# Batched matmul, 32 x (512x1024)·(1024x768): the few-row transfers moved from the first store to the last row tile of the first x, which is transposed late

## The chip, the cores and the metric

One core of a Trainium2 chip. The metric is the device time of one execution in microseconds (us); most executions of a kernel agree within some 0.3%.

## The reference

```python
def setup_inputs():
    batch, m, k, n = 32, 512, 1024, 768
    return {"x": np.random.randn(batch, m, k).astype(np.float32),
            "weight": np.random.randn(batch, k, n).astype(np.float32)}

def reference(x, weight):
    return np.matmul(x, weight).astype(np.float32)
```

The kernel casts to bf16 on the way in. It has to read 168 MB and write 50 MB.

## The kernel before

PE is the matrix engine, DVE and ACT are the vector and scalar engines, POOL and SP issue transfers; sixteen DMA engines share the bytes of a transfer, and it has landed when the last share has. Each batch has four row tiles of 128 rows (MT = 4). A row tile is transposed on the PE, copied out by DVE, and multiplied. The first x is loaded in f32 from the SP queue; the other x in pairs, and all weights, are loaded with a cast from the POOL queue. "x of batches 5 and 6" below is one such pair. The parts that matter (cuts marked with `...`):

```python
w_pool = ctx.enter_context(tc.tile_pool(name="w", bufs=4))
x_pool = ctx.enter_context(tc.tile_pool(name="x", bufs=3))
xT_pool = ctx.enter_context(tc.tile_pool(name="xT", bufs=6))
out_pool = ctx.enter_context(tc.tile_pool(name="out", bufs=7))
...
def transpose_first(mt):
    xT = xT_pool.tile([P, JT, P, 2], BF16, name="xT")
    for h in range(2):
        pt = tpsum.tile([P, JT, P], F32, name="pt")
        for i in range(JT):
            nc.tensor.transpose(pt[:, i, :], x_first[:, mt, JT * h + i::KT], ident)
        nc.vector.tensor_copy(...)
    return xT
...
def store(b):
    cols = MT * N
    if b == SKEWED:                       # SKEWED = 0: the first store
        cols -= 512
        for first in range(0, 120, 20):
            for at in range(first, first + 4):
                rows = slice(at, first + 20, 4)
                nc.sync.dma_start(out_view[b, rows, cols:], outs[b][rows, cols:])
        nc.sync.dma_start(out_view[b, 120:, cols:], outs[b][120:, cols:])
    nc.gpsimd.dma_start(out=out_view[b, :, :cols], in_=outs[b][:, :cols])
...
x_first = x_pool.tile([P, MT, K], F32, name="x_sb")
nc.sync.dma_start(x_first, x_view[0])
load_w(0)
...                                       # ident
load_pair(1); load_w(1); load_w(2); load_pair(3)
for b in range(B):
    if b % 2 and b + AHEAD + 1 < B:       # AHEAD = 3
        ...
            load_pair(b + AHEAD + 1)
    if b + AHEAD < B:
        load_w(b + AHEAD)
    ...                                   # stores; transposes
    for pair in range(2):
        pm = banks()
        for half in range(2):
            matmuls(pm, half, xT[2 * pair + half], b, range(KT), False)
        evacuate(b, pair, pm)
```

POOL issues its transfers in this order, one after the other, each when its buffer is free. The third x pair needs the buffer of the first x; the weights of batch 4 need the buffer of the weights of batch 0.

Of the kernel before, what the change touches and what calls it, by code (L numbers as in the profile page):

```python
# [13 lines left out]
def kernel(  # L14
# [6 lines left out]
    nc = tc.nc  # L21
    B, M, K = x.shape
    _, _, N = weight.shape
    P = 128
    MT = M // P
    KT = K // P
# [3 lines left out]
    AHEAD = 3  # L30
    LATE = 4
    HELD = 3
    SKEWED = 0

    const = ctx.enter_context(tc.tile_pool(name="const", bufs=1))
    w_pool = ctx.enter_context(tc.tile_pool(name="w", bufs=4))
# [10 lines left out]
    x_view = x.rearrange("b (mi mo) k -> b mi mo k", mi=P)  # L47
    pair_view = x[1:B - 1].rearrange("(p r) (mi mo) k -> p (r mi) mo k", r=2, mo=2 * MT)
    out_view = out.rearrange("b (mi mo) n -> b mi (mo n)", mi=P)

    xs, ws, outs = {}, {}, {}

    def banks():
        return [mpsum.tile([P, 512], F32, name=f"pm{i}") for i in range(3)]

    def load_pair(b):

        xs[b] = x_pool.tile([P, 2 * MT, K], BF16, name="x_sb")
        nc.gpsimd.dma_start(out=xs[b], in_=pair_view[b // 2])  # L59

    def load_last():
        xs[B - 1] = x_pool.tile([P, MT, K], BF16, name="x_sb")
        nc.gpsimd.dma_start(out=xs[B - 1], in_=x_view[B - 1])  # L63

    def load_w(b):
        ws[b] = w_pool.tile([P, KT, N], BF16, name="w_sb")
        at = 0
        for n in CHUNKED.get(b, (KT,)):
            nc.gpsimd.dma_start(out=ws[b][:, at:at + n, :], in_=w_view[b, :, at:at + n, :])  # L69
            at += n  # L70
# [9 lines left out]
    def transpose_pair(b, mt):  # L80

        both = xT_pool.tile([P, 2, JT, P // 2, 2, 2], BF16, name="xT")
        for half in range(2):
            nc.vector.tensor_copy(  # L84
                both[:, :, :, :, half, :].rearrange("p b j i r -> p j b i r"),
                words(b, mt + MT * half).rearrange("p j (b i r) -> p j b i r", b=2, r=2),
            )
        return [both[:, r].rearrange("p j i h r -> p j (i h) r") for r in range(2)]

    def transpose_last(mt):  # L90
        xT = xT_pool.tile([P, JT, P, 2], BF16, name="xT")
        nc.vector.tensor_copy(  # L92
            xT.rearrange("p j m r -> p (j m r)"), words(B - 1, mt).rearrange("p j m -> p (j m)")
# [10 lines that stand above are left out]
            nc.vector.tensor_copy(  # L104
                xT[:, 2 * h:2 * h + 2].rearrange("p j m r -> p j r m"),
                pt.rearrange("p (j r) m -> p j r m", r=2),
            )
        return xT
# [8 lines left out]
    def matmuls(pm, half, xT, b, kos, together):  # L117
        for ko in kos:
            for i, (bank, at, off, size) in enumerate(SPLITS[half]):
                shares = half == 1 and i == 0  # L120
                nc.tensor.matmul(  # L121
                    pm[bank][:, at:at + size],
                    xT[:, ko // 2, :, ko % 2],
                    ws[b][:, ko, off:off + size],
                    start=(ko == 0 and not (together and shares)),
                    stop=(ko == KT - 1),
                    skip_group_check=together,
                )

    def evacuate(b, pair, pm):  # L130
        o = outs[b][:, pair * N2:(pair + 1) * N2]
        nc.scalar.copy(o[:, 0:512], pm[0])  # L132
        nc.vector.tensor_copy(o[:, 512:1024], pm[1])  # L133
        nc.scalar.copy(o[:, 1024:N2], pm[2])  # L134

    def store(b):
        cols = MT * N
        if b == SKEWED:

            cols -= 512  # L140
            for first in range(0, 120, 20):
                for at in range(first, first + 4):
                    rows = slice(at, first + 20, 4)
                    nc.sync.dma_start(out_view[b, rows, cols:], outs[b][rows, cols:])
            nc.sync.dma_start(out_view[b, 120:, cols:], outs[b][120:, cols:])
        nc.gpsimd.dma_start(out=out_view[b, :, :cols], in_=outs[b][:, :cols])  # L146

    with tc.manual_schedule():
        x_first = x_pool.tile([P, MT, K], F32, name="x_sb")
        nc.sync.dma_start(x_first, x_view[0])  # L150
        load_w(0)
        ident = const.tile([P, P], F32)
        make_identity(nc, ident)
        load_pair(1)
        load_w(1)
        load_w(2)
        load_pair(3)

        ready = {}
        pending = []  # L160
        for b in range(B):
            if b % 2 and b + AHEAD + 1 < B:
                if b + AHEAD + 1 == B - 1:
                    load_last()
                else:
# [3 lines that stand above are left out]
            if b <= B - LATE:  # L169
                if b > 0:  # L170
                    pending.append(b - 1)
                if b + AHEAD < B - HELD or b == B - LATE:
                    for at in pending:
                        store(at)
                    pending = []
            if b == B - 1:
                halves = [slice(pair * N2, (pair + 1) * N2) for pair in range(2)]
                nc.sync.dma_start(out_view[b - 1, :, halves[0]], outs[b - 1][:, halves[0]])
                for late in range(B - LATE, B - 2):
                    nc.sync.dma_start(out_view[late], outs[late])  # L180
                nc.sync.dma_start(out_view[b - 1, :, halves[1]], outs[b - 1][:, halves[1]])
            outs[b] = out_pool.tile([P, MT * N], F32, name="out_sb")
            if b == 0:
                xT = {mt: transpose_first(mt) for mt in range(MT)}
            elif b == B - 1:
                xT = {mt: transpose_last(mt) for mt in range(MT)}
            else:
                if b % 2:
                    for mt in range(MT):
                        ready[b, mt], ready[b + 1, mt] = transpose_pair(b, mt)  # L190
                xT = {mt: ready.pop((b, mt)) for mt in range(MT)}
            if b not in CHUNKED:
                for pair in range(2):
                    pm = banks()
                    for half in range(2):
                        matmuls(pm, half, xT[2 * pair + half], b, range(KT), False)
                    evacuate(b, pair, pm)
                continue
            pms = [banks() for _ in range(2)]
            at = 0  # L200
            for n in CHUNKED[b]:
                last = at + n == KT
                for mt in range(MT):
                    matmuls(pms[mt // 2], mt % 2, xT[mt], b, range(at, at + n), True)
                    if last and mt % 2 == 1:
                        pair = mt // 2
                        evacuate(b, pair, pms[pair])
                        if b == B - 1:
                            nc.sync.dma_start(out_view[b, :, halves[pair]], outs[b][:, halves[pair]])
                at += n  # L210
# [30 lines left out]
```

## Time and profile before

| | before |
|---|---|
| time, first three runs | 517.0 us (515.5 to 518.96) |
| span of the profiled execution, granted clock | 515.9 us, 0.942 |
| PE busy | 440.0 us, 85% |
| HBM traffic over the span | 423 GB/s |

The views that carry the argument stand in the prediction below. One more is needed: the timeline of the first 36 us of the kernel before, cut to three lines (start and length in us, engine, line, what, count, and in brackets the idle time of the engine before it and what ended it).

```profile
12.27 6.95 PE L103 MATMUL pt<-ident,x_sb 128*128 128x128 f32 x32 [12.27 <-DMA x_sb<-in_x_dram]
...
19.52 0.53 POOL L59 DMA_DIRECT2D x_sb<-in_x_dram  x1 [14.38 <-PE pt L103]
...
29.92 0.53 POOL L69 DMA_DIRECT2D w_sb<-in_weight_dram  x1 [9.87 <-PE pm L121]
```

The first x has landed at 12.3 us. When its last transpose is through, at 19.5 us, POOL issues the next x pair, and when batch 0 is multiplied, at 29.9 us, the weights of batch 4. At those two moments the loads issued by 5.1 us still have work for the DMA engines: the last of them lands at 56.4 to 58.1 us.

### The profile page before, as it was taken

Reading aid. Unit: us, or ns where it says so; the run is one execution under the profiler, and the core shown is the slowest. Engines: PE = TensorE matmul, PEld = TensorE weight load, DVE = VectorE, ACT = ScalarE, POOL = GpSimd, SP = SyncE. Lnnn points to the kernel's source line nnn. Section 1 sums busy time; section 2 is a strip of 40 time slices with the busy share of each in tenths; the row PEclk is TensorE's granted clock in tenths of the full one; section 3 lists DMA queues with packets and bytes.
Section 4 is the critical chain, followed back from the end, with each engine's and each line's share of the span. In section 5 each row is a group of like instructions: output and inputs, shape, how many; then the busy total and the mean of one; then the engine's idle time right before and its main releaser. Section 6 shows DMA issues by size and latency. Waiting matters only on the chain.

```text
span 515.9 us, 5853 instructions
## 1 busy us (share of the span) xinstructions
PE 440.0 (85%) x2576; PEld 279.6 (54%) x2576; DVE 129.9 (25%) x196; ACT 76.2 (15%) x129; POOL 43.8 (8%) x87
## 2 busy tenths in 40 slices
PE   0999969979799697996979979898797988999992
PEld 0665635646366364663646636464464644656661
DVE  0541412314132041320413204141041410404131
ACT  0012111111111111111111111111111111111211
POOL 3001000010000100001000010000001100011000
PEclk9999998989899798997999979999798997999998
DMA  8999999999999999999999999999999999999996
GB/s 255 217 219 215 221 255 293 211 279 274 272 283 211 283 268 275 279 213 293 260 273 273 224 295 246 280 278 235 299 233 275 279 250 300 214 277 215 289 426 276
DMA packets 12952, 135.63 MB, mean 263 GB/s; under 512 B 1536, under 2 KB 1536, under 8 KB 3328
## 3 DMA queue, kind: packets, MB, share of 16 engines
q0 software_dynamic: 11664, 126.62, 96.2%
q1 hardware_dynamic: 1264, 8.65, 4.2%
q8 instruction: 20, 0.33, 0.2%
q14 instruction: 4, 0.03, 0.0%
HBM read 167.77 MB, written 50.33 MB: 423 GB/s over the span
## 4 chain that ended last, share of the span: by engine, by line
PE 64%; DMA 21%; DVE 7%; another core or an unknown queue 6%; issue 1%; ACT 0%
PE pm L121 56%; DMA w_sb<-in_weight_dram 19%; PE pt L77 6%; DVE xT L84 4%; DMA x_sb<-in_x_dram 2%; DVE out_sb L133 2%; PE pt L103 1%; DVE xT L104 0%; DVE xT L92 0%; ACT out_sb L134 0%
## 5 line engine op out<-in xcount | busy, mean ns | idle before, releaser
L121 PE MATMUL pm<-w_sb,xT 128*128 128x256 bf16 (+1 forms) x2048 | 358.9, 339 | 43.3 <-DMA w_sb<-in_weight_dram 43.3
L121 PEld LDWEIGHTS <-xT 128*128 128x128 bf16 x2048 | 206.8, 101 | 190.8 <-DMA w_sb<-in_weight_dram 47.9
L133 DVE COPY out_sb<-pm 128x512 f32<-128x512 f32 x64 | 44.3, 691 | 351.4 <-PE pm L121 338.4
L77 PE MATMUL pt<-ident,x_sb 128*128 128x128 f32 x496 | 79.8, 302 | 10.5 <-DVE xT L84 10.2
L132 ACT COPY out_sb<-pm 128x512 f32<-128x512 f32 x64 | 37.5, 585 | 305.9 <-PE pm L121 290.7
L77 PEld LDWEIGHTS pt<-ident,x_sb 128*128 128x128 f32 x496 | 69.3, 209 | 21.5 <-DVE xT L84 18.7
L84 DVE COPY xT<-pt 128x1024 bf16<-128x1024 bf16 x120 | 77.4, 687 | 11.0 <-PE pt L77 11.0
L134 ACT COPY out_sb<-pm 128x512 f32<-128x512 f32 x64 | 37.5, 585 | 124.0 <-PE pm L121 123.9
L69 POOL DMA_DIRECT2D w_sb<-in_weight_dram x37 | 19.7, 533 | 298.2 <-PE pm L121 261.4
L146 POOL DMA_DIRECT2D out_dram<-out_sb x28 | 15.0, 536 | 81.7 <-DMA w_sb<-in_weight_dram 41.9
L103 PE MATMUL pt<-ident,x_sb 128*128 128x128 f32 x32 | 6.7, 362 | 12.5 <-DMA x_sb<-in_x_dram 12.3
L103 PEld LDWEIGHTS pt<-ident,x_sb 128*128 128x128 f32 x32 | 5.1, 205 | 13.9 <-issue 12.2
L59 POOL DMA_DIRECT2D x_sb<-in_x_dram x15 | 8.0, 533 | 45.0 <-DMA out_dram<-out_sb 30.6
L104 DVE CAST xT<-pt 128x512 bf16<-128x512 f32 x8 | 5.8, 736 | 14.2 <-PE pt L103 13.8
L92 DVE COPY xT<-pt 128x1024 bf16<-128x1024 bf16 x4 | 2.6, 686 | 0.2 <-PE pt L77 0.2
L132 ACT ACT_TABLE_LOAD x1 | 1.3, 1283 | 0.7 <-PEq L225 0.7
L63 POOL DMA_DIRECT2D x_sb<-in_x_dram x1 | 0.5, 528 | 6.7 <-DMA w_sb<-in_weight_dram 6.7
masks.py:199 POOL TENSOR_SCALAR_AFFINE_SELECT ident<-ident 128x128 f32<-128x128 f32 x1 | 0.3, 287 | 0.1
masks.py:197 POOL MEMSET ident<- 128x128 f32 x1 | 0.2, 223 | 0.0
L225 POOL MEMSET const-float32-0.0<- 128x1 f32 x1 | 0.1, 98 | 0.2 <-issue 0.2
L225 POOL MEMSET const-bfloat16-1.0<- 128x1 bf16 x1 | 0.1, 101 | 0.0
L225 POOL MEMSET const-uint8-127<- 128x1 uint8 x1 | 0.1, 101 | 0.0
(1 smaller groups left out, 0.1 us busy)
## 6 DMA issues: line engine op xcount, KB each, us to landing
w_sb<-in_weight_dram POOLq DMA_DIRECT2D x28, 1536.0 KB, 47.3
out_dram<-out_sb POOLq DMA_DIRECT2D x27, 1536.0 KB, 46.6
x_sb<-in_x_dram POOLq DMA_DIRECT2D x15, 2048.0 KB, 52.4
w_sb<-in_weight_dram POOLq DMA_DIRECT2D x7, 768.0 KB, 38.4
out_dram<-out_sb SPq DMA_DIRECT2D x4, 768.0 KB
out_dram<-out_sb SPq DMA_DIRECT2D x2, 1536.0 KB
x_sb<-in_x_dram SPq DMA_DIRECT2D x1, 2048.0 KB
out_dram<-out_sb POOLq DMA_DIRECT2D x1, 1280.0 KB, 48.7
```

What stands on the lines that cost most here:

```text
L59: nc.gpsimd.dma_start(out=xs[b], in_=pair_view[b // 2])
L69: nc.gpsimd.dma_start(out=ws[b][:, at:at + n, :], in_=w_view[b, :, at:at + n, :])
L77: nc.tensor.transpose(pt[:, j, :], pairs[:, mo, j::JT], ident)
L84: nc.vector.tensor_copy(both[:, :, :, :, half, :].rearrange("p b j i r -> p j b i r"), words(b, mt + MT * half).rearrange("p j (b i r) -> ...
L92: nc.vector.tensor_copy(xT.rearrange("p j m r -> p (j m r)"), words(B - 1, mt).rearrange("p j m -> p (j m)"))
L103: nc.tensor.transpose(pt[:, i, :], x_first[:, mt, JT * h + i::KT], ident)
L104: nc.vector.tensor_copy(xT[:, 2 * h:2 * h + 2].rearrange("p j m r -> p j r m"), pt.rearrange("p (j r) m -> p j r m", r=2),)
L121: nc.tensor.matmul(pm[bank][:, at:at + size], xT[:, ko // 2, :, ko % 2], ws[b][:, ko, off:off + size], start=(ko == 0 and not (together an ...
L132: nc.scalar.copy(o[:, 0:512], pm[0])
L133: nc.vector.tensor_copy(o[:, 512:1024], pm[1])
L134: nc.scalar.copy(o[:, 1024:N2], pm[2])
L146: nc.gpsimd.dma_start(out=out_view[b, :, :cols], in_=outs[b][:, :cols])
```

## The change

The even split of a transfer gives each of the 16 DMA engines the same bytes. Transfers of five rows run on five engines only (the first such store reports in five single steps at 35.98 to 36.30 us), and the kernel before uses 25 small stores, all but one of five rows, to take work from the other eleven. The change moves this tilt to the front, into the load of the first x, where 13 small transfers (one of four rows, twelve of five) do the same beside one even transfer of 64 rows, and makes the first store plain. So that PE need not wait for these slow small loads, the last row tile is transposed only when its matmuls are due. The tail of the diff is the late transposition alone.

```diff
-        nc.sync.dma_start(x_first, x_view[0])
+        nc.sync.dma_start(x_first[:, :MT - 1], x_view[0, :, :MT - 1])
+        few = [slice(at, first + 20, 4) for first in (0, 20, 40) for at in range(first, first + 4)]
+        for rows in (slice(64, P), slice(60, 64), *few):
+            nc.sync.dma_start(x_first[rows, MT - 1], x_view[0, rows, MT - 1])
...
-                        store(at)
+                        nc.gpsimd.dma_start(out=out_view[at], in_=outs[at])
...
-                xT = {mt: transpose_first(mt) for mt in range(MT)}
+                xT = {mt: transpose_first(mt) for mt in range(MT - 1)}
...
-                        matmuls(pm, half, xT[2 * pair + half], b, range(KT), False)
+                        mt = 2 * pair + half
+                        if mt not in xT:
+                            xT[mt] = transpose_first(mt)
+                        matmuls(pm, half, xT[mt], b, range(KT), False)
```

The function `store` with its small transfers goes (cut here).

More of the change, by code (lines that the diff above doesn't have):

```diff
@@ L32 @@
     HELD = 3
-    SKEWED = 0
     const = ctx.enter_context(tc.tile_pool(name="const", bufs=1))
@@ L134, in evacuate @@
         nc.scalar.copy(o[:, 1024:N2], pm[2])
-    def store(b):
-        cols = MT * N
-        if b == SKEWED:
-            cols -= 512
-            for first in range(0, 120, 20):
-                for at in range(first, first + 4):
-                    rows = slice(at, first + 20, 4)
-                    nc.sync.dma_start(out_view[b, rows, cols:], outs[b][rows, cols:])
-            nc.sync.dma_start(out_view[b, 120:, cols:], outs[b][120:, cols:])
-        nc.gpsimd.dma_start(out=out_view[b, :, :cols], in_=outs[b][:, :cols])
     with tc.manual_schedule():
         x_first = x_pool.tile([P, MT, K], F32, name="x_sb")
-        nc.sync.dma_start(x_first, x_view[0])
+        nc.sync.dma_start(x_first[:, :MT - 1], x_view[0, :, :MT - 1])
+        few = [slice(at, first + 20, 4) for first in (0, 20, 40) for at in range(first, first + 4)]
+        for rows in (slice(64, P), slice(60, 64), *few):
+            nc.sync.dma_start(x_first[rows, MT - 1], x_view[0, rows, MT - 1])
         load_w(0)
```

## The prediction

> **What bounds the kernel now.** I read the page's rows of DMA and HBM first, then the waits, then the chain that ended last in order of time, then the landings (the semaphore updates with which each of the 16 DMA engines reports its share of a transfer), and last the packet records.
>
> The page, rows of parts 2 and 3:
>
> ```profile
> DMA  8999999999999999999999999999999999999996
> ...
> q0 software_dynamic: 11664, 126.62, 96.2%
> q1 hardware_dynamic: 1264, 8.65, 4.2%
> ...
> HBM read 167.77 MB, written 50.33 MB: 423 GB/s over the span
> ```
>
> The reader is to see that the DMA engines are full from the second slice to the last but one: 218 MB in 515.9 us. q0 carries the transfers issued from POOL, q1 those issued from SP. The first slice is 8 because the first packet starts at 1.76 us; the last is 6 because some engines are done before others.
>
> The list of waits has two lines that carry the next point:
>
> ```profile
> POOL w_sb L69 <- PE pm L121: 261.4, 25, 14.7
> ...
> PE pm L121 <- DMA w_sb<-in_weight_dram: 43.3, 12, 5.4
> ```
>
> PE stands still 43.3 us in all for weights that have not landed, in twelve waits. PE is the follower and has slack. The first line looks like the opposite (the issue of a weight load waits for PE to free a buffer), but an issue is not a transfer. Page part 6:
>
> ```profile
> w_sb<-in_weight_dram POOLq DMA_DIRECT2D x28, 1536.0 KB, 47.3
> ```
>
> A load lands 47.3 us after its issue, although its packets are only 8 x 0.93 us on each engine. The rest is queue. An issue that comes 10 or 20 us later goes into a queue that is not empty yet.
>
> The chain, in order of time (start, length, what):
>
> ```profile
> 0.74 11.39 DMA x_sb<-in_x_dram
> ...
> 19.22 10.41 PE pm L121 x64
> 29.64 0.28 issue
> 29.92 46.32 DMA w_sb<-in_weight_dram
> ...
> 76.29 12.05 PE pm L121 x63
> ...
> 423.55 3.59 another core or an unknown queue
> 427.14 0.05 issue
> 427.19 12.93 PE pm L121 x63
> ```
>
> At 76.29 batch 4 waits for weights; the lines at 104.62, 135.83, 167.52, 200.57, 231.93, 265.25, 296.34, 392.43 and 423.55 are such waits too, of 2.7 to 4.1 us, one for each two batches. The last ends at 427.14. After it PE runs through, but the end is again the queue: the last store is issued at 506.90 and its sixteen shares land between 510.62 and 514.99. On the engine that lands last, the store before it landed at 513.15, and 1.84 us is just what 8 packets of 6 KB take (0.235 us each), so that engine never stood idle. On it PE could have been some 4 us later without moving the end. **The bound is the work of the most loaded DMA engine**, from 1.76 us to 514.99 us.
>
> **How unequal the engines are.** Take each transfer's sixteen landings less their mean. Up to 25 us they lie within 0.4 us of it. By 75 us five shares stand at +1.2 to +1.5 and most others near -0.8. At 489 us there are two at +2.7 and +3.2, four at +0.7 to +1.0, and the earliest at -2.3. The five arise while the 25 small stores of the first output run (issued 30.3 to 68.3 us). That is what these stores are for: they take the last 512 columns (256 KB) away from the usual even split.
>
> **What the Trainium skill says.** (1) "DMA: Bandwidth & Descriptors", section "Why a DMA increments its semaphore by 16 and not by 1": a transfer runs on the largest number k of engines up to 16 that divides the row count, on a hardware queue the k lowest-numbered ones, and the sequencer posts the missing 16 - k at once. The trace agrees on k: the first five-row store's semaphore moves at 31.55 us and then in five single steps, 35.98 to 36.30 us. Which five, no row tells; I take the page's word for engines 0 to 4. (2) Same page, "Queues, rings and completion order": an engine takes turns between its queues, a packet at a time. The trace agrees: from 5.6 us on, 16 KB packets of x (0.62 us) alternate with weight packets (0.93 us). A thing that I read from the trace alone: the 4-byte packet that reports the landing takes a turn of its own. A small store thus costs two turns, and one lands each 1.9 us between weight packets, each 2.5 us between x packets (1.23 us).
>
> **The change, part by part.**
>
> *Removed:* the 24 stores of five rows and one of eight, 2 KB a row. Engines 0 to 4 carried 25 rows, 50 KB, in place of 16 KB: +34 KB. Engines 5 to 7 carried 2 KB (-14), engines 8 to 15 nothing (-16 KB). The first store is one even transfer of 1.5 MB again.
>
> *Added:* the last row tile of the first x, 512 KB, has the same treatment. Evenly it is 8 rows of 4 KB, 32 KB per engine. Now rows 64 to 127 are even (4 rows, 16 KB), rows 60 to 63 go to engines 0 to 3 (4 KB), and twelve transfers of five rows put 12 rows, 48 KB, on engines 0 to 4. Sum: 68 KB on engines 0 to 3 (+36), 64 KB on engine 4 (+32), 16 KB on 5 to 15 (-16 KB). **The tilt is the one there was, to within 2 KB**, at 26.4 KB/us (16 KB in 0.62 us) under 0.1 us. Overheads: 25 small packets at 0.09 us and 25 reports at 0.02 before, against 12 or 13 at about 0.155 (a quarter of 0.62) and as many reports: within some 0.3 us on the five. So the most loaded engine has the same work, whichever it is. Total bytes are the same.
>
> *Moved, early part.* The first three tiles are 12 KB packets on q1, 8 per engine. Before, about five 16 KB packets were through when q0 joined at 5.6 us; that is 80 KB, over six of the new ones, so the remaining one or two need two turns more: landing near 8.5 us, against 12.1 us. PE starts 3.5 us sooner, transposes three tiles in 5.2 us (three quarters of 6.95 us) and then waits for weights, which land near 15 us. Three of four tiles take three quarters of 10.4 us, to about 23 us.
>
> *Moved, late part.* The even piece takes four packets and a report, five turns: near 13.5 us. Then on engines 0 to 3 thirteen small transfers need two turns each, 26 turns beside q0's packets. About six are still weights of batch 0, then 8 of 1.23 us (x of batches 1 and 2) and the rest 0.93 us, plus 13 x 0.18 us. The last lands near 13.5 + 8 x 1.23 + 18 x 0.93 + 2.3 less waits that fall on report packets: **about 39 to 42 us**. The fourth tile's transposes wait for it, so PE stands some 16 us and batch 0 ends near 45 us in place of 29.6 us: 40 + 2.7 of transposes and casts + 2.6 of matmuls.
>
> *What that costs.* The load of x for batches 5 and 6 is issued after the last transpose of the first x: near 42 us in place of 19.5. The weights of batch 4 go out near 45 in place of 29.9. But the loads issued before 5 us keep the engines busy to 58 us (the fourth weights landed at 58.1), so q0 doesn't run dry; the margin falls from 28 to some 13 us. PE then has batches 1 to 3 to do and reaches batch 4 near 88 in place of 76.3 us. With 3 to 4 us of slack per two batches it should be level again by about 170 us.
>
> Sum: DMA work unchanged, no empty queue, PE delay absorbed: 0 us, give or take 0.5. The median before is 517.0, the mean of the three runs 517.2. I say **516.7 us**.
>
> **Rivals.** (a) *PE's late start reaches the end.* For it: PE is busy 85%, its delay is some 15 us, and full-rate running may be met by the throttle (PEclk falls to 8 in some slices). Against: 43.3 us of waits to absorb it, and the tail where PE could be 4 us later. If half of it got through: 524 us. (b) *The queue runs dry near 58 to 70 us*, since POOL issues in order and stands behind the x load. Each us without packets is a us at the end: 520 to 527 us. For it: my landing estimate could be 10 us short; if even the first three tiles waited for the small transfers, batch 0 would end near 57 us. Even then the late loads come about when the queue ends. (c) *The tilt gains:* the most loaded engine is relieved sooner or loses the overheads of 25 small stores: 515 to 516.5 us. The early landings say that an engine's order of work is free, so I expect nothing over 0.5 us. (d) *The sooner start of PE helps:* only if PE were the bound at the start; but the first weights land near 15 us anyway.
>
> **Range and chances.** The runs before spread from 515.5 to 518.96 us; (c) gives the low side, (a) and (b) the high side: 514.5 to 519.5 us. A gain over 2% would need 10 us of DMA work to vanish, and no byte does: 0.01. A loss over 2% needs (a) or (b) nearly whole: 0.03.
>
> **What would show it.** Right: DMA slices still 9 through the span; small x transfers landing one per 2 us to about 40 us; a PE idle of some 16 us before the fourth tile's transposes; first transposes near 8.5 us; PE's total wait for weights lower by about the same 15 us; waits for weights returning after some 170 us; spread of landings at the end as before, about 5.5 us. Wrong: a slice near 60 us with DMA under 9, no PE waits left at 400 us, or a two-late-engines pattern that has changed, which would mean that the tilt does not reach the engines I think it does.

## The result

| | before | after |
|---|---|---|
| time, median of 6 runs | 516.35 us (515.49 to 518.96) | 519.97 us (519.35 to 520.59) |
| ratio | | 1.0065 (1.0041 to 1.009) |
| span of the profiled execution | 515.9 us | 518.6 us |
| granted clock | 0.942 | 0.961 |

A ratio is the mean time of one kernel's fast runs over that of the other's of the same rounds, so it is not quite the ratio of the medians. Of 516.35 us, 0.41 to 0.9% is 2.1 to 4.6 us. The change costs some 3.4 us in the mean, clear of noise; within 2%, as predicted, but above the predicted range (514.5 to 519.5 us).

The same timeline after the change:

```profile
0.74 0.38 SPq L138 DMA_DIRECT2D x_sb<-in_x_dram  x1
1.18 25.09 SPq L141 DMA_DIRECT2D x_sb<-in_x_dram  x14
...
39.91 5.45 PE L102 MATMUL pt<-ident,x_sb 128*128 128x128 f32 x24 [39.91 <-DMA x_sb<-in_x_dram]
...
54.34 0.53 POOL L58 DMA_DIRECT2D x_sb<-in_x_dram  x1 [49.20 <-PE pt L102]
...
57.50 0.53 POOL L68 DMA_DIRECT2D w_sb<-in_weight_dram  x1 [2.63 <-PE pm L120]
```

The third of these lines is the surprise. The 24 transposes of the first three tiles, whose data landed by 10.2 us, start at 39.91 us, just after the last of the small loads has landed (39.7 us). The x pair goes out at 54.34 us in place of 19.52, the weights of batch 4 at 57.50 in place of 29.92.

What did they wait for? The view of line 102, which is the transposes of the first x:

```profile
L102 PEldq EVENT_SEMAPHORE  x4: 51/51/51, 35.7 to 39.8; - x4
```

Four wait instructions, the last at 39.8 us, all stand ahead of the first transpose (the last transposes run at 53.8 us and have none of their own). In the trace's records each names two semaphores, together all eight that the SP loads report to. So in the program as it was built, every transpose of the first x, even of tile 0, waits for every piece. In the run with neighbouring rows, below, the same view has a fifth wait, at 10.2 us, that names the semaphore of the first load alone:

```profile
L102 PEldq EVENT_SEMAPHORE  x5: 51/51/51, 10.2 to 39.8; - x5
```

The windows of 56 to 60 us, before and then after (columns: window, its length, busy time and count of PE, PEld, DVE, ACT and POOL, granted clock, DMA share, GB/s; packets count where they start, so a short window's share may pass 1):

```profile
56.00:58.00 2.00, 1.70 (x14) 1.47 (x12) 1.88 (x3) 0.58 (x1) 0.53 (x1) 1.00 1.20 258
58.00:60.00 2.00, 1.82 (x13) 1.59 (x12) 1.63 (x3) 0.00 (x0) 0.54 (x1) 1.00 1.05 225
```

```profile
56.00:58.00 2.00, 2.00 (x16) 1.60 (x13) 0.98 (x2) 0.59 (x1) 0.50 (x1) 1.00 0.91 178
58.00:60.00 2.00, 1.51 (x11) 1.14 (x9) 1.76 (x4) 0.00 (x0) 0.56 (x2) 1.00 0.95 197
```

The queue has run dry for a moment: 178 GB/s in place of 258. Eleven engines had landed the loads of the start by 56.0 to 56.5 us, and the first packets of the pair issued at 54.34 us start on them at 55.75 to 57.22 us: the issue came a little too late. The five that carry the small loads were busy to 58.4 us. So the dry moment took its time from the eleven, and with it the tilt: at 57 us five shares landed 1.1 to 1.5 us after the mean of their transfer, at 67 us no share is over 0.7. The last share of the pair lands at 68.10 us, with neighbouring rows at 68.08.

How much was lost, and when? I take the mean of the sixteen landings of a transfer, which doesn't depend on the spread of the engines. For the weights of batch 5, by when both kernels have moved the same bytes, it is 85.15 us before and 87.22 us after: **2.1 us lost by then**. Of these some 0.6 us are the dry moment and its restart (the x pair issued at 54.34 lands at a mean of 67.40 us; in the runs below that have the small loads and a queue that was never dry, at 66.7 to 66.8). The other 1.5 us lie in the next transfer, the weights of batch 4: 8.8 us after the pair in place of 7.2. Its packets at 70 to 75 us take up to 2.2 us each in place of 0.93, although the queue is not empty then. At the end of this trace the last store lands 2.4 us later in the mean than before, in a second trace of the same kernel (below) 1.2 us: most of what is lost early stays, with a drift of about a us either way.

And PE? Three lines of the waits after:

```profile
POOL x_sb L58 <- PE pt L102: 49.2, 1, 49.2
...
PE pt L102 <- DMA x_sb<-in_x_dram: 39.9, 1, 39.9
...
PE pm L120 <- DMA w_sb<-in_weight_dram: 25.4, 8, 5.7
```

PE lost 39.9 us at the start and still waits for weights 25.4 us in all later: it has caught up in full. In the timeline its first such wait comes at 205.6 us, and from then on it follows the weights again. PE's delay as such did not reach the end; the late issues did, as the runs with deeper queues show below. Nor was it the throttle that rival (a) feared: the granted clock was 0.961, over the 0.942 of before.

### The profile page after: what moved, and what is told of

The parts are those of the page before. It is cut to its first block, busy times and chain, and to the rows that moved or that the text cites. A ratio compares the mean times of both kernels' runs of the same rounds, so it can differ in the third digit from the quotient of the medians.

```text
span 518.6 us, 5792 instructions
## 1 busy us (share of the span) xinstructions
PE 429.1 (83%) x2528; PEld 277.3 (53%) x2576; DVE 129.7 (25%) x196; ACT 76.3 (15%) x129; POOL 43.8 (8%) x87
## 4 chain that ended last, share of the span: by engine, by line
PE 61%; DMA 26%; DVE 6%; another core or an unknown queue 3%; issue 1%; SPq 1%; ACT 0%
PE pm L120 54%; DMA w_sb<-in_weight_dram 19%; DMA x_sb<-in_x_dram 7%; PE pt L76 6%; DVE xT L83 4%; DVE out_sb L132 2%; PE pt L102 1%; SPq L141 1%; DVE xT L103 0%; DVE xT L91 0%; ACT out_sb L133 0%; SPq L138 0%
## 5 line engine op out<-in xcount | busy, mean ns | idle before, releaser
L120 PE MATMUL pm<-w_sb,xT 128*128 128x256 bf16 (+1 forms) x2000 | 348.4, 333 | 28.3 <-DMA w_sb<-in_weight_dram 25.4
L120 PEld LDWEIGHTS <-xT 128*128 128x128 bf16 x2048 | 204.3, 100 | 167.6 <-DMA w_sb<-in_weight_dram 28.5
L102 PE MATMUL pt<-ident,x_sb 128*128 128x128 f32 x32 | 6.5, 372 | 39.9 <-DMA x_sb<-in_x_dram 39.9
L102 PEld LDWEIGHTS pt<-ident,x_sb 128*128 128x128 f32 x32 | 5.2, 206 | 41.0 <-issue 39.9
```

The lines of the kernel that those rows point to most:

```text
L120: nc.tensor.matmul(pm[bank][:, at:at + size], xT[:, ko // 2, :, ko % 2], ws[b][:, ko, off:off + size], start=(ko == 0 and not (together an ...
```

## The experiments

Theory A: the transposes of all tiles were held back because the framework that places the waits cannot tell the strided row pieces (every fourth row) from the rest of the tile. PE came 28 us late, so the two loads that wait for PE were issued late, and the DMA queue ran dry. Rival B: the small loads or the tilt cost the time themselves. Rival E: PE's lateness is too much to absorb.

### Neighbouring rows in place of every fourth

```diff
-few = [slice(at, first + 20, 4) for first in (0, 20, 40) for at in range(first, first + 4)]
+few = [slice(5*n, 5*n+5) for n in range(12)]
```

> The changed kernel with the twelve five-row pieces of the last row tile cut as five neighbouring rows each, in place of every fourth row; same row counts, same number of transfers, all else as changed. Theory A (the transposes of the first three tiles were held back to 39.9 us because the framework could not tell strided row slices apart from the rest of the tile; PE came late, the loads that wait for PE were issued late, and the queue ran dry near 56 us): first transposes near 8.8 us, fourth tile's near 40 us, batch 0 ends near 45 us, no dip of DMA near 56 us, 516.5 us (515.5 to 517.5). Rival B (the small loads or the tilt at the start cost the time themselves): 520 us as in the changed kernel, whatever PE does.

Measured: 516.3 us, ratio to before 1.0007 (0.9971 to 1.0042). The timeline:

```profile
10.27 5.84 PE L102 MATMUL pt<-ident,x_sb 128*128 128x128 f32 x24 [10.27 <-DMA x_sb<-in_x_dram]
15.90 8.27 PE L120 MATMUL pm<-w_sb,xT 128*128 128x512 bf16 x47
...
39.89 1.95 PE L102 MATMUL pt<-ident,x_sb 128*128 128x128 f32 x8 [15.71 <-DMA x_sb<-in_x_dram]
...
42.13 0.53 POOL L58 DMA_DIRECT2D x_sb<-in_x_dram  x1 [36.98 <-PE pt L102]
...
45.85 0.53 POOL L68 DMA_DIRECT2D w_sb<-in_weight_dram  x1 [3.19 <-PE pm L120]
```

The small loads are as many and as large, and the last lands at 39.7 us as before. But the first three tiles are transposed from 10.27 us and only the fourth waits. The issues at 42 and 46 us still find a full queue; the weights of batch 5 land at a mean of 85.06 us. The small loads and the tilt cost nothing that 0.4% would show (B falls), and neither does a PE gap of 15.7 us. PE's first wait for weights comes back at 167.5 us.

### The last row tile in a tile of its own

```diff
+        x_late = xT_pool.tile([P, K], F32, name="xT")
...
-            nc.sync.dma_start(x_first[rows, MT - 1], x_view[0, rows, MT - 1])
+            nc.sync.dma_start(x_late[rows], x_view[0, rows, MT - 1])
```

> The changed kernel, the rows still every fourth one, but the last row tile of the first x in a tile of its own, so that the transposes of the other three cannot wait for it. Theory A: as with neighbouring rows, first transposes near 8.8 us, 516.5 us (515.5 to 517.5). Rival B: 520 us.

Measured: 516.96 us, ratio 1.0012 (0.9975 to 1.0049). The rows are every fourth again, yet the first transposes start at 10.33 us, because the strided pieces are now alone in their tile; the weights of batch 5 land at a mean of 85.02 us. This and the run above differ from the changed kernel in what waits for what (here the x pair need not even wait for the fourth tile and goes out at 16.17 us), and both have the time of before.

### No tilt at all

```diff
-        nc.sync.dma_start(x_first[:, :MT - 1], ...)   # and the 14 small loads
+        nc.sync.dma_start(x_first, x_view[0])
```

> The changed kernel with the first x loaded in one even transfer as before, and no small transfers at all; only the late transposes stay. It measures the tilt: theory A says that the tilt is small and the same in both kernels. If the latest engines at the end are among those that the tilt relieves (5 to 15), they get 16 KB more: 0.6 us over the kernel before, 517 us. If they are among the five loaded ones, they get 34 KB less: 1.3 us under it, 515 us. Rival C (the small transfers of either kernel cost several us in turns): under 514 us.

Measured: 516.29 us, ratio 1.0003 (0.9972 to 1.0035). This is the kernel before without its small stores, with the late transposes. Together they are worth nothing measurable here. The tilt, the purpose of the transfers that the change moves, neither gains nor costs within 0.35% (1.8 us); a fraction of a us, as the expectation has it, could not be seen.

### PE late by the same 16 us, without small loads

The kernel before with the last row tile as one even transfer from POOL behind the third weights, transposed late.

```diff
+        nc.gpsimd.dma_start(out=x_first[:, MT - 1], in_=x_view[0, :, MT - 1])   # after load_w(2)
```

> The kernel before with its small stores, but the last row tile of the first x goes as one even transfer on the POOL queue behind the third weights, and is transposed late. No small loads; PE waits for it until about 41 us and batch 0 ends near 46 us. The prediction's own claim is that such a delay of 16 us is absorbed: 516.5 us (515.5 to 517.5). Rival D (any late PE costs, by some 0.1 us for each us, because the first 150 us are never caught up): 518 us or more.

Measured: 518.13 us, ratio 1.0033 (1.0001 to 1.0066). This one is not clean. The fourth tile is transposed at 40.29 us, batch 0 ends near 46.8, the queue is not dry, and the weights of batch 5 land at a mean of 85.12 us, as without a delay. So nothing was lost in the first 85 us, but the runs were 1.7 us slower in the mean, just clear of zero. The runs with neighbouring rows and with a tile of its own, with the same delay, were not. In the first of them and here, the executions near 518 us have the lowest granted clock (0.935, 0.936) and the fastest the highest (0.941, 0.942); which causes which is not shown. I leave it open.

### A deeper queue, with and without the change

Five weight buffers in place of four, six output buffers in place of seven; weights are loaded one batch further ahead. In the kernel before and in the changed one:

```diff
-w_pool = ctx.enter_context(tc.tile_pool(name="w", bufs=4))
+w_pool = ctx.enter_context(tc.tile_pool(name="w", bufs=5))
-out_pool = ctx.enter_context(tc.tile_pool(name="out", bufs=7))
+out_pool = ctx.enter_context(tc.tile_pool(name="out", bufs=6))
...
         load_pair(3)
+        load_w(3)
...
-            if b + AHEAD < B:
-                load_w(b + AHEAD)
+            if b + AHEAD + 1 < B:
+                load_w(b + AHEAD + 1)
```

> The kernel before with five weight buffers in place of four and six output buffers in place of seven, so that the fourth weights are loaded in the first 6 us too. A control for the next run: the queue was never empty in the kernel before, so 516.3 us (515 to 518).

> The changed kernel with the same five weight and six output buffers. The transposes still wait for all small loads, to about 40 us, and batch 0 still ends near 57 us, but the queue now holds one more load of 7.4 us, to about 66 us, when the next load is issued at 54 us. Theory A (the dry queue is the cost, not PE's lateness): no dip of DMA at 56 us, within 1 us of its control. Rival E (PE 28 us late is too much to absorb, whatever the queue does): 3 us over its control, with PE's waits for weights gone.

Measured: 515.22 us for the control, ratio 0.9977 (0.9948 to 1.0005), and 515.44 us for the changed kernel, ratio 0.998 (0.9948 to 1.0011). From the changed kernel's waits and its windows at 56 to 60 us:

```profile
PE pt L102 <- DMA x_sb<-in_x_dram: 39.9, 1, 39.9
```

```profile
56.00:58.00 2.00, 2.00 (x15) 1.59 (x13) 1.06 (x2) 0.58 (x1) 0.53 (x1) 1.00 1.11 233
58.00:60.00 2.00, 1.51 (x10) 1.21 (x9) 1.76 (x4) 0.00 (x0) 0.54 (x1) 1.00 1.08 229
```

The transposes wait as long as before, and the x pair is issued as late (54.27 us). But the queue holds one more load, there is no dip, and the change costs nothing. E falls: a PE that starts 28 us late is absorbed when the queue lasts.

### One more x buffer in the changed kernel

```diff
-x_pool = ctx.enter_context(tc.tile_pool(name="x", bufs=3))
+x_pool = ctx.enter_context(tc.tile_pool(name="x", bufs=4))   # xT 6 -> 5, out 7 -> 6
```

> The changed kernel with four buffers for x (and six for the output, five for the transposed x, to make room). The transposes still wait to 39.9 us and the weights of batch 4 still go out near 57 us, but the x of batches 5 and 6 no longer waits for a buffer and is loaded with the first loads, so the queue lasts to about 67 us. Theory A: no dip at 56 us, the early loss of 2.1 us gone, 516.5 us (515 to 518). Rival E (PE's lateness): 520 us.

Measured: 517.01 us, ratio 1.0003 (0.9961 to 1.0046). The transposes wait to 39.90 us and the weights of batch 4 go out at 58.12, later than in the changed kernel. Only the x pair goes out with the first loads, at 5 us. That is enough: the queue lasts, and the weights of batch 4 land at a mean of 73.97 us in place of 76.18. So it is the x pair, whose buffer the transposes held, that came too late. The early loss is not quite gone, as I had expected: the weights of batch 5 land at 85.91 us, 0.8 us after those of the kernel before, with packets stretched at 82 to 84 us. Later the trace makes that up, and the time shows no loss.

### A longer dry moment, without small loads

The kernel before with the even last row tile behind the fourth weights, at the end of the first loads, transposed late.

```diff
                 load_w(b + AHEAD)
+            if b == 0:
+                nc.gpsimd.dma_start(out=x_first[:, MT - 1], in_=x_view[0, :, MT - 1])
```

> The kernel before with the last row tile of the first x in one even transfer at the very end of the first loads, behind the fourth weights, transposed late. No small loads and no strided rows, but the load that waits for its transposes is issued near 61 us, after the queue has ended near 59.5 us. Theory A: a dip of DMA near 60 us, deeper than the changed kernel's, some 3 us lost, 519 to 522 us. Rival B (the small loads are the cost): 516.5 us.

Measured: 522.2 us, ratio 1.0118 (1.0082 to 1.0154). Its windows from 54 to 62 us:

```profile
54.00:56.00 2.00, 0.00 (x0) 0.00 (x0) 0.00 (x0) 0.00 (x0) 0.00 (x0) 0.50 0.89 268
56.00:58.00 2.00, 0.76 (x4) 0.79 (x5) 0.00 (x0) 0.00 (x0) 0.00 (x0) 0.50 0.23 92
58.00:60.00 2.00, 2.00 (x10) 1.23 (x9) 1.46 (x2) 0.00 (x0) 0.52 (x1) 0.50 0.00 0
60.00:62.00 2.00, 2.00 (x8) 0.99 (x7) 0.00 (x0) 0.00 (x0) 0.01 (x1) 0.50 0.93 139
```

No load or store packet starts between 58 and 60 us. The weights of batch 5 land at a mean of 91.48 us, 6.3 us later than in the kernel before, and the runs are 1.18% of 517 us, 6.1 us (4.2 to 8.0), longer in the mean. So an early loss of the DMA engines is found again at the end in about its size, but not one for one in each execution: the traced one, the fastest of the four, has the last store land 5.1 us later in the mean than the kernel before, and its span is 3.8 us longer. I had expected 3 us of loss; the tile landed at 57.1 us and the queue was dry earlier than I had put it.

### The changed kernel again, and with its first store held back

> The changed kernel unchanged, for a second trace. Its first one shows, besides the dip at 56 us, weight packets stretched at 70 to 75 us by 1.3 us in the mean of the engines. If that belongs to the kernel it is there again; if it was chance it is elsewhere or absent. Time 520 us.

Measured: 519.0 us (one run). The second trace repeats the first: the weights of batch 5 at a mean of 87.21 us, a dip at 56 us, and stretched packets at 70 to 75 us.

```diff
-                if b + AHEAD < B - HELD or b == B - LATE:
+                if b != 1 and b + AHEAD < B - HELD or b == B - LATE:
```

> The changed kernel with the first store held back by one batch, so that it no longer stands behind the weights of batch 4 in the queue. It asks what stretches the packets of these weights at 70 to 75 us, in both traces of the changed kernel. If the store behind them does it, they are not stretched here; if it is an aftermath of the dry queue, they are, by 1.2 to 1.5 us. The queue may run dry again near 75 us, so the time says little: 519 to 521 us.

Measured: 522.54 us (one run, its queue dry a second time near 74 us). The weights of batch 4 are no longer stretched: 7.3 us after the x pair. The weights of batch 5, which now stand ahead of the first store, are: packets at 80 to 84 us take 1.6 us longer in the mean of the engines. So in these traces the stretching goes with the weights just ahead of the first store in the queue. That isn't all of it: in the neighbouring-rows run the weights of batch 4 stand ahead of the first store too and take 7.2 us, in the run with four x buffers it is the weights behind the first store that are stretched (8.1 us), and without any tilt, with a queue that never ran dry, those of batch 4 take 7.9 us. So it is not the dry queue alone either, though it was largest after one. What it is stays open.

### Something that beats both?

The deep queue again with more rounds, and the deep queue without small stores:

```diff
-        if b == SKEWED: ...               # the small stores, on top of the deeper queue
```

> The same with the small stores of the kernel before, again and with more rounds, beside it: 515.3 us. The first time it was 0.2% under the kernel before with an interval that just reaches zero; if the gain is real it is under it again and clear of zero.

> The kernel before with five weight and six output buffers and with no small transfers at all: the first x in one even load, the first store in one even transfer. The tilt was worth nothing in the kernel with four weight buffers, so the time should be that of its control with the tilt, 515.3 us (514 to 516.5), some 1 us under the kernel before and 4.5 under the changed one. If the small stores cost anything once PE is well ahead, it is under 514.5 us.

Measured: 515.52 us, ratio 0.9991 (0.9963 to 1.002), and 516.49 us, ratio 1.0004 (0.9982 to 1.0026). The gain of the first try is not confirmed. No version is faster than the kernel before clear of noise.

## Why the prediction was wrong

**The bound: right in the main.** The work of the DMA engines sets the time. The long dry moment shows it best: 6.3 us lost early, 6.1 us at the end in the mean of the runs. That it is the work of the most loaded engine is not shown: taking the tilt away changed nothing that could be measured.

**The tilt unchanged and worth nothing in the difference: right in its worth.** Without any tilt the ratio to before is 1.0003. The tilt itself was as predicted to 57 us, and then the dry moment undid it.

**The small loads land at one per two turns, the last at 39 to 42 us: right.** The last landed at 39.7 us.

**"PE starts 3.5 us sooner, transposes three tiles in 5.2 us": this step failed.** I took it that a transpose waits for the bytes that it reads, and the built program has it wait for all fifteen loads. The first transpose came at 39.91 us, not near 8.5. Where the framework does tell the pieces apart, with neighbouring rows, PE starts at 10.27 us. (8.5 was itself 1.8 us early: two of the sixteen engines needed one turn more for their share, to 10.2 us.) In that kernel the rest of the prediction holds closely: a gap of 15.7 us for the predicted 16, the x pair issued at 42.13 us for 42, the weights at 45.85 for 45, PE level with the weights at 167.5 us for 170, and 516.3 us for 516.7.

**"q0 doesn't run dry; the margin falls from 28 to some 13 us": failed with it.** The x pair went out 12 us later than I had worked out, which ate up the margin, and the queue of eleven engines ended at about 56 us. Rival (b) had it: "if even the first three tiles waited for the small transfers, batch 0 would end near 57 us". It ended at 57.0. I dismissed it with "even then the late loads come about when the queue ends". About was not enough: x pair and weights went out at 54.3 and 57.5 us, and two traces show 2.1 us lost by 87 us. The sign that I had set for it, a slice near 60 us with DMA under 9, did not come: the page has 9 there, for a slice is 13 us long and the dip 2 to 4.

**The size.** These 2.1 us are the low edge of the interval of the measured loss, 2.1 to 4.6 us. Where the rest of the 3.4 us of the means lies I could not locate: the two traced executions of the changed kernel have spans 2.7 and 1.3 us longer than the traced one of the kernel before, and executions of that kernel alone differ by up to 4.0 us (514.43 to 518.43 in one set of runs). Of the 2.1 us, 1.5 are stretched packets that no rival had.

**The delay of PE is absorbed: right,** even at 28 us, as the deeper queue shows.

## What to carry to other kernels

After cutting a load into pieces, look in the trace at what the first reader waits for before counting on an early start: strided row pieces can make every reader of the tile wait for every piece, and neighbouring rows or a tile of their own avoid it. Where DMA was the bound, here, a compute engine 28 us late cost nothing measurable by itself; ask which loads wait for a buffer that it holds, and whether the queue lasts until they have been issued and their packets start, which after the long dry moment took 1.3 to 2.3 us.

## What the Trainium skill lacked or had wrong

- "DMA: Bandwidth & Descriptors" says that an engine takes turns between its queues by packets. It doesn't say that the 4-byte packet that reports a landing takes a turn of its own: the five-row stores of the kernel before landed one each 1.9 us between packets of 0.93 us, though their own data took 0.09 us.
- No page has it that waits can cover more than the bytes read: row pieces with a step of 4 in a tile made transposes of other columns wait to 39.91 us; pieces of five neighbouring rows let them start at 10.27 us.
- No page has the cost of a restart after a dry queue: the first x packets after it took up to 1.9 us in place of 1.23 in the changed kernel; after the long dry moment up to 2.3 us, and the engines' first packets started 1.3 to 2.3 us after the issue.
- No page explains the stretched weight packets near the first store, up to 2.2 us in place of 0.93 in two traces of the changed kernel, and fewer of them in other runs.
- The page's remark that engines 7 and 15 are usually slower could not be tried, for the traces don't number the engines. Two late shares show in some traces and not in others: the last store's two latest land 2.3 and 2.9 us after the mean of its shares in the kernel before, and 1.1 and 1.3 us in the first run with the deeper queue.
